# Attention probabilities turned by crossbar DMA as float16 halves, scores and values in float16 halves, two heads side by side in the value products

## The chip, the cores and the metric

The kernel runs on one core of one Trainium2 chip. The metric is the device time of one execution in microseconds (us); lower is better. The core has a matrix engine (PE, with weight loads shown apart as PEld), VectorE (DVE), ScalarE (ACT), GpSimd (POOL) and SyncE (SP), each with its own in-order queue. The kernel issues nearly all of its DMAs from SP.

## What is computed

One layer of a streaming encoder works on 1,024 prompt frames and 32 sample frames of 1,024 channels. The input is normalised, projected by nine weight groups, and goes through two branches: causal attention with 16 heads of 64 channels, and a depthwise convolution of width 31. Both are gated, projected, mixed and projected once more. The part that matters here is the attention of the prompt (the reference, cut):

```python
def fox_attend(q, k, v, cq, ck, qpos, kpos):
    s = jnp.einsum('bqhd,bkhd->bhqk', q.astype(jnp.float32), k.astype(jnp.float32))
    bias = jnp.transpose(cq, (0, 2, 1))[:, :, :, None] - jnp.transpose(ck, (0, 2, 1))[:, :, None, :]
    mask = qpos[:, None] >= kpos[None, :]
    s = jnp.where(mask[None, None], s + bias, jnp.finfo(jnp.float32).min)
    p = jax.nn.softmax(s, axis=-1)
    o = jnp.einsum('bhqk,bkhd->bqhd', p, v.astype(jnp.float32))
    return o.astype(v.dtype)
...
for i in range(T // Q_BLOCK):
    lo, hi = i * Q_BLOCK, (i + 1) * Q_BLOCK
    blocks.append(fox_attend(q[:, lo:hi], k[:, :hi], v[:, :hi], c[:, lo:hi], c[:, :hi],
                             jnp.arange(lo, hi), jnp.arange(hi)))
```

A block of 128 queries `i` of a head looks at the first `128 * (i + 1)` keys, so a head has 36 tiles of 128 queries by 128 keys.

## The kernel before

The program has five stages. First x is normalised and turned. Then come the projections of the convolution input, of v, k, q and of the gate `ga`, with the convolution's taps on DVE (`conv_taps`, L377) between them. Then comes the attention stage, then the output projections "pa" and "pb" (L186, called by `outproj`), then the last product (L1537). A projection multiplies float16 halves: a weight is split into `wh` and `wl`, x into `xh` and `xl`, and each 128x352 output tile collects 8 times 3 matmuls (`mms`, L186).

In the attention stage 22 gate projections (`filler`, `gate_steps`) are woven in as filler: one call of `fill(1)` runs one step of three matmuls (128x352 each), 24 steps make a gate. Each such step is also one beat that paces the taps on DVE and the splitting of the next weights (`wl` on DVE at L144, `wh` on POOL at L139).

The stage goes through a list `seq` of 128 blocks (16 heads of 8 query blocks) and four `Sample` items for the 32 sample frames. For each block:

- `scores` (L1150, L1151): two products into PSUM `psS`, one of 128 rows for the cross terms of the q and k halves (QB, KB) and one of 68 rows for the high halves and the cumulative log gates (QA, KA). The tiles are float32 rounded for the matrix engine. A block of 128 keys is computed 256 wide.
- `top` (L1157, L1159): DVE adds the causal mask to the diagonal tile and takes the row maximum.
- `soft` (L1166): ACT takes the exponential into SBUF tile `P` and sums the rows.
- `norm` (L1171, L1172): DVE takes the reciprocal, POOL scales `P`.
- `turn` (L1186, L1189): PE transposes the 128x128 tiles of `P` in float32 into PSUM; ACT or DVE copies them to the SBUF tiles `pt`.
- `values` (L1205 to L1214): once per head, 20 float32 products 64 channels tall; tile `j` writes the upper or the lower half of the PSUM partitions by whether `j` is even or odd, ACT copies one half and DVE adds the other, and every second head POOL multiplies by the gate `ga`, and the tile goes to DRAM `s_o`.

The order of PE, SP, DVE and ACT in this stage is the order in which the code is written (`manual_schedule`): block `n` is turned while block `n + 3` is scored, with filler after it. q, k and v pass through DRAM in float32 (`s_q`, `s_k`, `s_v`), and `Head.load` brings them back by eight DMAs a head. A DMA on SP uses one of eight semaphores in turn and so waits for the DMA eight places ahead of it.

## Time and profile before

| what | value |
|---|---|
| time, median of 3 runs | 1330.91 us (1329.0, 1330.91, 1336.58) |
| profiled execution, first to last instruction | 1331.8 us |
| granted clock of PE, mean | 0.996 of full |
| busy share PE / DVE / ACT / POOL | 98% / 74% / 52% / 42% |
| attention stage in the trace | 566.5 to 1041.8 us |
| DMA, whole span | 194.96 MB, mean 146 GB/s |

The profiled execution took 1331.8 us from its first to its last instruction; the profile shows nothing around that, and the span lies 0.9 us above the median of the three runs. In the profile a line such as "L186 PE MATMUL pj<-xl,wh" names the line of the kernel, the engine, the operation, and the tile written and the tiles read. Matmuls are pipelined, so the duration of one is longer than the distance to the next; costs on PE are read from the distance between starts.

### The profile page before, as it was taken

To read this page: it belongs to the slowest core of one execution; us is meant where nothing else is said; L and a number is where in the kernel's file an instruction comes from. 1 tells how busy PE (TensorE), PEld (TensorE's weight loads), DVE (VectorE), ACT (ScalarE), POOL (GpSimd) and SP (SyncE) were. 2 spreads that over 40 slices of the span, in tenths; PEclk is the share of its full clock that TensorE was granted. 3 is DMA by queue.
4 is the path that set the end of the run, shared out by engine and by line. 5 is a ranking of instruction groups with operands and counts; after the bars stand their busy time and mean duration, and the time that the engine had idled before them with its cause. 6 is when DMAs were issued, how large, how long until landed. Compare 5 with 4: busy or idle time off the path is not lost.

```text
span 1331.8 us, 24835 instructions
## 1 busy us (share of the span) xinstructions
PE 1311.1 (98%) x9396; PEld 1004.7 (75%) x9396; DVE 986.0 (74%) x1513; ACT 693.1 (52%) x1336; POOL 565.2 (42%) x597
## 2 busy tenths in 40 slices
PE   8999999999999999999899999999999999999999
PEld 5687876666666666677577767767777699999998
DVE  6797879889999998897787875754555388176664
ACT  5644545767686843455545555555555466233320
POOL 4001014637475730245445544342443258255562
PEclk8999999999999999999999999999999999999999
DMA  6243243425252553526545654465561788434461
GB/s 253 99 137 109 86 121 112 146 63 198 86 187 65 186 156 130 164 69 165 147 119 142 181 142 121 114 187 134 150 170 39 247 320 275 157 130 143 126 214 67
DMA packets 113495, 194.96 MB, mean 146 GB/s; under 512 B 34080, under 2 KB 80032, under 8 KB 113376
## 3 DMA queue, kind: packets, MB, share of 16 engines
q1 hardware_dynamic: 113232, 193.31, 46.9%
q8 instruction: 74, 1.21, 0.4%
q14 instruction: 45, 0.37, 0.1%
q10 hardware_dynamic: 144, 0.07, 0.0%
HBM read 127.68 MB, written 65.64 MB: 145 GB/s over the span
## 4 chain that ended last, share of the span: by engine, by line
PE 88%; DVE 7%; ACT 2%; issue 1%; DMA 1%; SPq 1%; POOL 0%; DVEq 0%; ACTq 0%; POOLq 0%
PE pj L186 59%; PE pjv L785 6%; PE pj L1537 6%; PE po L1205 5%; PE ptr L1186 4%; PE psS L1151 2%; PE psS L1150 2%; DVE y L377 2%; DVE wl L144 1%; DVE nm L1159 1%; DMA s_y<-y 1%; PE pst L884 1%; PE pst L885 0%; DMA ga<-s_ga 0%; PE ptx L586 0%
## 5 line engine op out<-in xcount | busy, mean ns | idle before, releaser
L186 PE MATMUL pj<-xl,wh 128*128 128x352 f16 (+2 forms) x1536 | 481.7, 314 | 1.8 <-DVE xl L593 1.6
L186 PE MATMUL pj<-xh,wh 128*128 128x352 f16 (+2 forms) x1536 | 482.2, 314 | 0.8 <-DVE qn L919 0.6
L186 PE MATMUL pj<-xh,wl 128*128 128x352 f16 (+2 forms) x1536 | 481.7, 314 | 0.0
L186 PEld LDWEIGHTS <-wh 128*128 128x128 f16 x3072 | 301.6, 98 | 161.7 <-issue 8.1
L377 DVE SCALAR_TENSOR_TENSOR y<-u,vec_t,y 128x1086 f32<-128x1086 f32 x240 | 348.5, 1453 | 12.1 <-ACT y L374 9.0
L1172 POOL TENSOR_SCALAR P<-P,nm 128x128 f32<-128x128 f32 (+7 forms) x128 | 140.9, 1101 | 203.3 <-DVE nm L1171 181.9
L186 PEld LDWEIGHTS <-wl 128*128 128x128 f16 x1536 | 150.8, 98 | 71.0 <-issue 1.4
L1166 ACT ACTIVATE P<-psS,nm 128x128 f32<-128x128 f32 (+7 forms) x128 | 95.1, 743 | 129.1 <-DVE nm L1171 111.8
L144 DVE SCALAR_TENSOR_TENSOR wl<-raw,sc,wh 128x384 f16<-128x384 f32 x188 | 133.3, 734 | 16.3 <-ACT wh L141 15.8
L1159 DVE TENSOR_REDUCE nm<-psS 128x1 f32<-128x128 f32 (+7 forms) x128 | 97.0, 758 | 10.7 <-POOL P L1172 0.5
L1186 PE MATMUL ptr<-ident,P 128*128 128x128 f32 x576 | 87.2, 274 | 9.8 <-DVE pt L1189 4.7
L1189 ACT COPY pt<-ptr 128x512 f32<-128x512 f32 (+3 forms) x128 | 64.4, 503 | 44.6 <-PE ptr L1186 44.3
L178 POOL TENSOR_TENSOR wl<-raw,wh 128x384 fp32r<-128x384 f32 (+1 forms) x51 | 60.9, 1221 | 61.8 <-ACT wh L175 46.7
L904 POOL TENSOR_TENSOR sql<-sqf,sqh 128x352 fp32r<-128x352 f32 x48 | 57.7, 1203 | 64.9 <-ACT sqh L901 64.9
L1186 PEld LDWEIGHTS ptr<-ident,P 128*128 128x128 f32 x576 | 69.0, 141 | 19.3 <-POOL rstd L357 3.7
L1150 PE MATMUL psS<-KB,QB 128*128 128x256 f32 (+2 forms) x192 | 81.6, 426 | 0.0
L120 POOL CAST topb<-tops 128x2 bf16<-128x2 f32 x35 | 18.6, 532 | 135.9 <-ACT junk L117 86.0
L1205 PE MATMUL po<-pt,V 128*64 128x256 f32 x640 | 72.6, 382 | 2.6 <-ACT pts L1107 2.6
L930 POOL TENSOR_TENSOR ql<-qn,qh 128x352 fp32r<-128x352 f32 (+1 forms) x48 | 67.6, 1424 | 6.1 <-ACT qh L929 6.0
L785 PE MATMUL pjv<-vwh,xh 128*128 128x260 f16 x256 | 70.1, 274 | 0.0
L785 PE MATMUL pjv<-vwl,xh 128*128 128x260 f16 x256 | 70.0, 273 | 0.0
L785 PE MATMUL pjv<-vwh,xl 128*128 128x260 f16 x256 | 69.9, 273 | 0.0
(277 smaller groups left out, 2572.1 us busy)
## 6 DMA issues: line engine op xcount, KB each, us to landing
raw<-wf SPq DMA_DIRECT2D x92, 512.0 KB
QB<-s_q SPq DMA_DIRECT2D x32, 256.0 KB
KB<-s_k SPq DMA_DIRECT2D x32, 256.0 KB
kT<-qn SPq DMA_DIRECT2D x8, 528.0 KB
s_ga<-t SPq DMA_DIRECT2D x24, 176.0 KB
s_gb<-t SPq DMA_DIRECT2D x24, 176.0 KB
s_ma<-t SPq DMA_DIRECT2D x24, 176.0 KB
s_mb<-t SPq DMA_DIRECT2D x24, 176.0 KB
```

The lines of the kernel that those rows point to most:

```text
L144: nc.vector.scalar_tensor_tensor(wl[:, ks, :], raw[:, ks, :], self.s[:, i:i + 1], wh[:, ks, :], op0=ALU.mult, op1=ALU.subtract)
L186: nc.tensor.matmul(ps, a[:, kt, :], b(kt, sl), start=(first and n == 0), stop=(last and n == N - 1))
L377: t = nc.vector.scalar_tensor_tensor(y, u[:, i:i + CW], w, y, op0=ALU.mult, op1=ALU.add)
L785: nc.tensor.matmul(ps[:, :VC], a, b, start=(n == 0), stop=(n == 23))
L930: nc.gpsimd.tensor_sub(ql[:, :n], qn[:, o], f32(qh[:, :n]))
L1150: nc.tensor.matmul(ps[:, b, :wm], QB[:, qsl], KB[:, ksl], start=True, stop=False)
L1159: nc.vector.tensor_reduce(nm[:, 0:1], ps[:, :nb, :w], axis=AX.XY, op=ALU.max, negate=True)
L1166: nc.scalar.activation(P[:, :nk].rearrange("p (b w) -> p b w", b=nb), ps[:, :nb, :w], AF.Exp, bias=nm[:, 0:1], accum_out=nm[:, 1:2])
L1172: nc.gpsimd.tensor_scalar(P[:, :nk], P[:, :nk], nm[:, 2:3], 1.0, op0=ALU.mult, op1=ALU.mult)
L1186: nc.tensor.transpose(pt[:, 128 * j:128 * j + 128], P[:, 128 * (4 * u + j):128 * (4 * u + j) + 128], ident)
L1205: nc.tensor.matmul(po[rows], V[:, j, :], parts[c][:, j, :], start=(c % 2 == 0 and j < 2), stop=(c % 2 == 1 and j >= 2 * c))
L1537: nc.tensor.matmul(pss[c][:, :HC], a[:, k, :], x, start=(not more and kt == 0 and n == 0), stop=(kt == 3 and n == 2), skip_group_check=more)
```

## The change

Everything between q, k, v and the attention output is stored as pairs of float16 halves, high and low. The DRAM copies of q and k become float16. The cumulative log gates become three float16 parts, so that the product of the high halves has 70 rows. A power of two moves between the gains of q and k so that both fit float16 (`gains`, `balance`); k is scaled back for its output (`unscaled`). v is stored as two float16 tensors `vh` and `vl`.

Heads are treated in pairs. A `Unit` is a query block `i` of head `e` of the pair, and 128 units run in the order pair, block, head. `Unit.scores` computes only the keys that exist and adds the causal mask by a matmul with a scaled identity (`identm`, `masks[0]`). After the exponential, `factor` makes the reciprocal times 2^14, `high` (ACT) writes the high half of the scaled probabilities, and `low` writes the low half: by one DVE instruction for the even head, by two POOL instructions for the odd head. `turn` is one DMA per unit that transposes both halves from `PH` to `PT` in the crossbar; there are no transposes on PE and no copies from PSUM. `Pair2.values` makes the products of a pair for 256 queries: three float16 products (high by high, low by high, high by low) for each key tile and each head, with head 0 in PSUM partitions 0 to 63 and head 1 in 64 to 127, one after the other in program order. `gated` scales on ACT and multiplies by the gate on POOL.

The loop issues, for unit `k`: its scores, the factor and high half of unit `k - 1`, half of the filler, its maximum and exponential, the low half of unit `k - 1`, the events of that step (loads, value products, sample work), the other half of the filler, and the transposing DMA of unit `k - 2`. Filler is dealt out in proportion to a unit's width plus 320; 30 of the 528 filler steps are kept for the end. The value products of a pair's block pair `m` stand `LAG` = 5 steps behind its last unit.

The diff, cut to its core (left out are the power of two between q and k, the mask constants, the sample's tile names and the loads of the first heads):

```diff
--- before.py
+++ after.py
...
+PS14 = 2.0 ** 14
+LAG = 5
+WB = 320
...
-    s_q = dram.tile([2, D, T], F32, name="s_q")
-    s_k = dram.tile([2, D, T], F32, name="s_k")
-    s_v = dram.tile([8, 128, D], F32, name="s_v")
+    s_q = dram.tile([2, D, T], F16, name="s_q")
+    s_k = dram.tile([2, D, T], F16, name="s_k")
+    s_v = dram.tile([2, 8, 128, D], F16, name="s_v")
...
-            nc.sync.dma_start(s_v[t, :, 256 * c:256 * c + 256], vf)
+            vh, vl = [vp.tile([128, 256], F16, name=n, tag=n, bufs=3) for n in ("vh", "vl")]
+            vx = vp.tile([128, 256], F32, name="vx", tag="vx", bufs=2)
+            nc.scalar.mul(vh, ps[:, :256], 2.0 ** -15)
+            nc.gpsimd.tensor_scalar(vx, vf, vsc[:, c:c + 1], 1.0, op0=ALU.mult, op1=ALU.mult)
+            nc.gpsimd.tensor_sub(vl, vx, vh)
+            for n, x in enumerate((vh, vl)):
+                nc.sync.dma_start(s_v[n, t, :, 256 * c:256 * c + 256], x)
...
+            (0.5, lambda: V.tensor_scalar(rc, cc, 1.0 / CU, None, op0=ALU.mult)),
+            (0.5, lambda: V.tensor_copy(cp3[:, 0, :], rc)),
+            (0.8, lambda: V.tensor_sub(rc, rc, cp3[:, 0, :])),
+            (0.5, lambda: V.tensor_copy(cp3[:, 1, :], rc)),
+            (0.8, lambda: V.tensor_sub(cp3[:, 2, :], rc, cp3[:, 1, :])),
+            (0.8, lambda: V.tensor_scalar(cn3, cp3, -1.0, None, op0=ALU.mult)),
...
+            ql = tp.tile([128, CH], F16, name="ql", tag="ql")
+            nc.gpsimd.tensor_sub(ql[:, :n], qn[:, o], qh[:, :n])
+            nc.sync.dma_start(dst[0, f * 128:(f + 1) * 128, o], qh[:, :n])
+            nc.sync.dma_start(dst[1, f * 128:(f + 1) * 128, o], ql[:, :n])
+                    kun = tp.tile([128, TT], F32, name="kun", tag="kun", bufs=1)
+                    def unscaled():
+                        nc.scalar.mul(kun, qn, bal[:, 1:2])
+                        nc.sync.dma_start(kT[f], kun)
...
+    class Heads:
...
+                QA, QB, KA, KB = [hp.tile([n, T], F16, name=f"{a}{e}", tag=f"{a}{e}", bufs=2)
+                                  for a, n in (("QA", 70), ("QB", 128), ("KA", 70), ("KB", 128))]
+                for t, src, low, c in ((QB, s_q, 0, s_aq), (KB, s_k, 64, s_ak)):
+                    nc.sync.dma_start(t[low:low + 64], src[1, hs, :])
+                    nc.sync.dma_start(t[64 - low:128 - low], src[0, hs, :])
+                for t, src, c in ((QA, s_q, s_aq), (KA, s_k, s_ak)):
+                    nc.sync.dma_start(t[0:64], src[0, hs, :])
+                    nc.sync.dma_start(t[64:70], c[h])
+                self.q.append((QA, QB, KA, KB))
...
+            self.V = [hp.tile([128, 8, 128], F16, name=n, tag=n, bufs=2) for n in ("Vh", "Vl")]
+            for n, t in enumerate(self.V):
+                nc.sync.dma_start(t, s_v[n, :, :, 128 * self.g:128 * self.g + 128].rearrange("b t d -> t b d"))
...
+    class Unit:
...
-            QA, QB, KA, KB = self.head.q
...
-            ps = psS.tile([128, 2, 512], F32, name="psS", tag="S")
-            nb = 1 if nk <= 512 else 2
-            for b in range(nb):
-                ksl = slice(b * w, b * w + wm)
-                nc.tensor.matmul(ps[:, b, :wm], QB[:, qsl], KB[:, ksl], start=True, stop=False)
-                nc.tensor.matmul(ps[:, b, :wm], QA[:, qsl], KA[:, ksl], start=False, stop=True)
+            self.ps = ps = psS.tile([128, T], F32, name="psS", tag="S")
+            for k0 in range(0, w, 512):
+                ksl = slice(k0, min(k0 + 512, w))
+                last = ksl.stop == w
+                nc.tensor.matmul(ps[:, ksl], QB[:, qsl], KB[:, ksl], start=True, stop=False)
+                nc.tensor.matmul(ps[:, ksl], QA[:, qsl], KA[:, ksl], start=False, stop=not last)
+            nc.tensor.matmul(ps[:, w - 128:w], identm, masks[0], start=False, stop=True)
...
-            diag = ps[:, nb - 1, w - 128:w]
-            nc.vector.tensor_add(diag, diag, cmask)
-            nm = ap.tile([128, 3], F32, name="nm", tag="nm", bufs=6)
-            nc.vector.tensor_reduce(nm[:, 0:1], ps[:, :nb, :w], axis=AX.XY, op=ALU.max, negate=True)
+            self.nm = ap.tile([128, 3], F32, name="nm", tag="nm", bufs=6)
+            nc.vector.tensor_reduce(self.nm[:, 0:1], self.ps[:, :self.w], axis=AX.X, op=ALU.max, negate=True)
...
+        def factor(self):
+            nm = self.nm
             nc.vector.reciprocal(nm[:, 2:3], nm[:, 1:2])
-            nc.gpsimd.tensor_scalar(P[:, :nk], P[:, :nk], nm[:, 2:3], 1.0, op0=ALU.mult, op1=ALU.mult)
+            nc.vector.tensor_scalar(nm[:, 2:3], nm[:, 2:3], PS14, None, op0=ALU.mult)
+
+        def high(self):
+            n = self.i + 1
+            self.H = ap.tile([128, 8, 2, 128], F16, name="PH", tag="PH", bufs=3)
+            self.P3 = self.P[:, :self.w].rearrange("p (j k) -> p j k", j=n)
+            nc.scalar.mul(self.H[:, :n, 0, :], self.P3, self.nm[:, 2:3])
+
+        def low(self):
+            n = self.i + 1
+            f = self.nm[:, 2:3]
+            if self.e:
+                nc.gpsimd.tensor_scalar(self.P3, self.P3, f, 1.0, op0=ALU.mult, op1=ALU.mult)
+                nc.gpsimd.tensor_sub(self.H[:, :n, 1, :], self.P3, self.H[:, :n, 0, :])
+            else:
+                nc.vector.scalar_tensor_tensor(self.H[:, :n, 1, :], self.P3, f, self.H[:, :n, 0, :],
+                                               op0=ALU.mult, op1=ALU.subtract)
 
...
-                pt = psT.tile([128, 512], F32, name="ptr2", tag="T")
-                for j in range(nj):
-                    nc.tensor.transpose(pt[:, 128 * j:128 * j + 128],
-                                        P[:, 128 * (4 * u + j):128 * (4 * u + j) + 128], ident)
...
-                for j in range(2 * c + 2):
-                    rows = slice(64 * (j % 2), 64 * (j % 2) + 64)
-                    nc.tensor.matmul(po[rows], V[:, j, :], parts[c][:, j, :], start=(c % 2 == 0 and j < 2),
-                                     stop=(c % 2 == 1 and j >= 2 * c))
...
+            i, e, m = self.i, self.e, self.i // 2
+            if i % 2 == 0 and e == 0:
+                self.pair.pt[m] = ap.tile([128, 2, 2, 2 * m + 2, 2, 128], F16, name="PT", tag=f"PT{m % 2}", bufs=1)
+            out = self.pair.pt[m][:, i % 2, e, :i + 1, :, :].rearrange("p j n q -> p (j n) q")
+            nc.sync.dma_start_transpose(out, self.H[:, :i + 1, :, :].rearrange("p j n k -> p (j n k)"))
...
+            Vh, Vl = self.hd.V
+            for j in range(2 * m + 2):
+                ii = slice(1 if j == 2 * m + 1 else 0, 2)
+                for n, (v, x) in enumerate(((Vh, 0), (Vl, 0), (Vh, 1))):
+                    for e in range(2):
+                        nc.tensor.matmul(po[64 * e:64 * e + 64, 128 * ii.start:256], v[:, j, 64 * e:64 * e + 64],
+                                         pt[:, ii, e, j, x, :], start=(j == 0 and n == 0),
+                                         stop=(j == 2 * m + 1 and n == 2))
+            self.po = po
...
+    def fill_for(x):
+        share["want"] += x
+        n = int(share["want"]) - share["done"]
+        share["done"] += n
+        fill(n)
+
+    rate = (24 * NFILL - 30) / sum(u.w + WB for u in units)
...
+    for g, p in enumerate(duos):
+        t = 16 * g
+        if g + 1 < len(duos):
+            at(t + 2, duos[g + 1].hd.load)
+            at(t + 5, duos[g + 1].hd.load_v)
+        for m in range(4):
+            k = t + 4 * m + 3 + LAG
+            at(k - 4, lambda p=p, m=m: p.load_gate(m))
+            at(k, lambda p=p, m=m: p.values(m))
...
+    for k in range(len(units) + 2):
+        u = units[k] if k < len(units) else None
+        last = units[k - 1] if 0 < k <= len(units) else None
+        if u:
+            u.scores()
+        if last:
+            last.factor()
+            last.high()
+        fill_for(rate * (u.w + WB) / 2 if u else 2.0)
+        if u:
+            u.top()
+            u.soft()
+        if last:
+            last.low()
+        for fn in events.pop(k, ()):
+            fn()
+        fill_for(rate * (u.w + WB) / 2 if u else 2.0)
+        if k > 1:
+            units[k - 2].turn()
+    for k in sorted(events):
+        fill(5)
+        for fn in events.pop(k):
+            fn()
...
```

PE before, in the attention stage where the scores of a two-tile block stand ahead of the transposes of a seven-tile one (QB, KB, QA, KA are the halves of q and k, P the probabilities, ident the identity, pj the filler's output):

```order
L186 MATMUL pj<-xl,wh 128x352
L1150 MATMUL psS<-KB,QB 128x256
L1151 MATMUL psS<-KA,QA 128x256
L1186 MATMUL ptr_8895<-ident,P 128x128 x4
L1186 MATMUL ptr_8901<-ident,P 128x128 x3
L186 LDWEIGHTS wh
```

PE after, at a unit of two key tiles (`identm` is the scaled identity, `mask` the causal mask):

```order
L190 MATMUL pj<-xl,wh 128x352
L1198 LDWEIGHTS QB_8593
L1198 MATMUL psS<-KB_8595,QB_8593 128x256
L1199 LDWEIGHTS QA_8592
L1199 MATMUL psS<-KA_8594,QA_8592 128x256
L1200 LDWEIGHTS identm
L1200 MATMUL psS<-mask_180,identm 128x128
L190 LDWEIGHTS wh
```

The transposes behind the scores are gone, every score product has a weight load row of its own, and a 128x128 product adds the mask.

SP before, where a head is loaded (raw is a weight tile for the filler, s_ma a gate's output):

```order
L969 DMA s_ma<-t 128x352
L984 DMA QB<-s_q 64x1024
L985 DMA QB<-s_q 64x1024
L986 DMA KB<-s_k 64x1024
L987 DMA KB<-s_k 64x1024
L988 DMA QA<-s_q 64x1024
L989 DMA QA<-s_aq 4x1024
L990 DMA KA<-s_k 64x1024
L991 DMA KA<-s_ak 4x1024
L1194 DMA ga<-s_ga 128x1024
L109 DMA raw<-wf 128x1024
```

SP after, behind the sixteen loads of a pair, of which the last five are shown (PH and PT are the probabilities ahead of and behind the crossbar):

```order
L1038 DMA KB_8595<-s_k 64x1024
L1040 DMA QA_8592<-s_q 64x1024
L1041 DMA QA_8592<-s_aq 6x1024
L1040 DMA KA_8594<-s_k 64x1024
L1041 DMA KA_8594<-s_ak 6x1024
L1238 DMA_TRANSPOSE PT<-PH 128x2x128 x2
L1248 DMA ga<-s_ga 128x256
L1018 DMA s_gb<-t 128x352
L1238 DMA_TRANSPOSE PT<-PH 128x4x128
L1268 DMA s_o<-ot 128x256
L1047 DMA Vh<-s_v 128x8x128
L1047 DMA Vl<-s_v 128x8x128
```

The loads of two heads now stand in one run, and the transposing DMAs of the next units stand behind them in the same queue, between stores and loads.

DVE before, in the later part of the stage (nm holds maximum, sum and reciprocal):

```order
L144 SCALAR_TENSOR_TENSOR wl<-raw,sc,wh 128x384
L1210 TENSOR_TENSOR ot<-ot,po 64x512 x2
L144 SCALAR_TENSOR_TENSOR wl<-raw,sc,wh 128x256
L1157 TENSOR_TENSOR psS<-psS,cmask 128x128
L1159 TENSOR_REDUCE nm<-psS 128x1
L1171 RECIPROCAL nm<-nm 128x1
```

DVE after, at two units (PH is the low half that DVE writes for the even head):

```order
L1214 RECIPROCAL nm<-nm 128x1
L1215 TENSOR_SCALAR nm<-nm 128x1
L1204 TENSOR_REDUCE nm<-psS 128x1
L1230 SCALAR_TENSOR_TENSOR PH<-P,nm,PH 128x6x128
L1214 RECIPROCAL nm<-nm 128x1
```

The mask addition and the copies from PSUM are gone, the reciprocal of unit k - 1, which reads the sum of its exponential, stands ahead of the maximum of unit k, and each second unit has a pass over its probabilities.

257 lines of the change are left out of this document (104 added, 153 removed).

## Prediction

> **What bounds the kernel now.** I read the page's engine totals first, then the busy times by stage, then the issue times of single PE instructions, and last the other engines in the stage that the change touches.
>
> ```profile
> span 1331.8 us, 24835 instructions
> PE 1311.1 (98%) x9396; PEld 1004.7 (75%) x9396; DVE 986.0 (74%) x1513; ACT 693.1 (52%) x1336; POOL 565.2 (42%) x597
> ...
> 46.50:566.50 520.00, 519.45 (x3725) 361.16 (x3724) 458.68 (x526) 303.00 (x558) 193.44 (x192) 1.00 0.41 131
> 566.50:1041.80 475.30, 462.92 (x3458) 336.40 (x3457) 323.47 (x682) 251.19 (x572) 207.68 (x254) 1.00 0.49 134
> 1041.80:1246.70 204.90, 204.90 (x1298) 197.56 (x1299) 116.61 (x134) 89.76 (x119) 103.58 (x79) 1.00 0.60 208
> ```
>
> The columns of the stages are length, busy time of PE, PEld, DVE, ACT and POOL, granted clock, DMA share and GB/s. PE is the bound everywhere. The attention stage is 475.3 us long with 12.4 us in which PE is idle; DVE has 68% of it, ACT 53%, POOL 44%. Work taken off PE there shortens the stage, until DVE or a transfer is in the way. The granted clock is 1.00, so cost is instructions.
>
> Costs on PE come from the distances between starts:
>
> ```profile
> 513.47 21.50 PE pj L186 x144
> 956.57 4.47 PE po L1205 x40
> ...
> 914.46 0.39 PE L1150 MATMUL psS<-KB,QB 128*128 128x512 f32 x1
> 914.69 0.40 PE L1151 MATMUL psS<-KA,QA 68*128 68x512 f32 x1
> 914.93 0.71 PE L1186 MATMUL ptr<-ident,P 128*128 128x128 f32 x5
> 915.48 0.31 PE L186 MATMUL pj<-xh,wh 128*128 128x352 f16 x1
> ...
> L186 PE MATMUL pj<-xh,wh 128*128 128x352 f16 x529 | 166.2, 314 | 0.0
> L1186 PE MATMUL ptr<-ident,P 128*128 128x128 f32 x576 | 87.2, 274 | 9.8 <-DVE pt L1189 4.7 <-ACT pt L1189 2.4 <-DVE os_t L1131 1.5
> L1205 PE MATMUL po<-pt,V 128*64 128x256 f32 x640 | 72.6, 382 | 2.6 <-ACT pts L1107 2.6
> ```
>
> A float16 matmul of 352 columns takes 21.50 / 144 = 0.149 us, 0.424 ns a column. Three times 529 of them in the stage are 237 us of filler, and they stay. A score matmul of 512 columns takes 0.235 us (914.46 to 914.93 for two), 0.459 ns a column. A transpose takes (915.48 - 914.93) / 5 = 0.11 us, so 576 take 63.4 us. A record of the value products takes 4.47 / 40 = 0.112 us, so 640 take 71.5 us.
>
> **The change part by part.** *Transposes.* All 576 leave PE: -63.4 us.
>
> *Scores.* Before, a head has 4,736 columns (blocks below 256 are computed 256 wide) in two products: 9,472 x 0.459 ns = 4.35 us. After, 4,608 columns twice and eight masks of 128 are 10,240 x 0.424 ns = 4.34 us. I count no difference: the narrower blocks pay for the mask.
>
> *Value products.* A pair has 6 x 4,608 = 27,648 float16 columns in 120 matmuls; eight pairs are 221,184 columns. One after the other that is 93.8 us, 22 more than now. Two side by side, in the two halves of the array, it is 46.9. Does the array do that?
>
> ```profile
> 807.23 0.76 PE L1235 MATMUL psn<-mean,ones_f 128*128 128x352 f32 x2
> ...
> 909.23 0.65 PE L1119 MATMUL po<-vc,pts 128*32 128x64 f32 x32
> 909.70 0.29 PE L1119 MATMUL po<-pts 128*32 128x64 f32 x8
> ```
>
> L1235 is float32 at full width: one record lasts 459 ns in its group, so the second starts 0.30 us after the first, 0.85 ns a column. At that rate a 256-column record of L1205 would take 0.218 us; it takes 0.112. The old products, which alternate between the halves too, already run two at a time. I take 46.9: -24.6, with +22 as the other end.
>
> Against this stands the Trainium skill, "TensorE: Matmul & The Clock Gate", section "The mechanism": a weight load overlaps running matmuls only where the row groups differ, and both heads use all rows. By that rule the products would not gain, and the sum would be that of the third rival. The trace doesn't bear it out: L1119 starts 32 products with 32 loads, all on full rows, in 0.47 us, 15 ns each.
>
> PE's work becomes 462.9 - 63.4 - 24.6 = 375 us. With the idle time of now the stage would be 387.
>
> *What is late next: DVE.*
>
> ```profile
> L1159 DVE TENSOR_REDUCE nm<-psS 128x1 f32<-128x128 f32 (+7 forms) x128 | 97.0, 758 | 10.7 <-POOL P L1172 0.5
> L377 DVE SCALAR_TENSOR_TENSOR y<-u,vec_t,y 128x1086 f32<-128x1086 f32 x46 | 67.5, 1466 | 2.3 <-ACT y L374 2.2
> L144 DVE SCALAR_TENSOR_TENSOR wl<-raw,sc,wh 128x384 f16<-128x384 f32 (+1 forms) x66 | 43.9, 683 | 0.4 <-POOL wh L139 0.4
> L1157 DVE TENSOR_TENSOR psS<-psS,cmask 128x128 f32<-128x128 f32 x128 | 37.4, 292 | 28.7 <-PE psS L1151 28.5
> L1189 DVE COPY pt<-ptr 128x128 f32<-128x128 f32 (+1 forms) x64 | 31.2, 488 | 43.9 <-PE ptr L1186 43.7
> L1210 DVE TENSOR_TENSOR ot<-ot,po 64x512 f32<-64x512 f32 x31 | 21.2, 685 | 53.8 <-ACT ot L1209 53.8
> L1171 DVE RECIPROCAL nm<-nm 128x1 f32<-128x1 f32 x128 | 19.7, 154 | 0.1
> ...
> 600.00:700.00 100.00, 93.33 (x705) 66.31 (x702) 77.19 (x141) 50.86 (x115) 48.55 (x54) 0.98 0.55 144
> 700.00:800.00 100.00, 97.95 (x740) 71.52 (x737) 77.89 (x149) 53.61 (x120) 53.49 (x56) 1.00 0.55 153
> ```
>
> DVE loses L1157, L1189 and L1210, 89.8 us. It gains 128 small factors at the 154 ns of L1171, 19.7 us, and 64 low halves of 576 columns on average: 0.78 us each by L377 (1.35 ns a column), 1.03 by L144 (1.78 for 384), so 50 to 66; I take 58. That is 323.5 - 89.8 + 19.7 + 58 = 311 us, 80% of 387. It isn't spread evenly: the 46 taps come at 0.2 a filler step, within 230 of the 528 steps, the first 44%. There DVE has (311 - 67.5) x 0.44 + 67.5 = 175 us against 0.44 x 387 = 170 us of PE. DVE can't be full: the factor of unit k - 1 waits for that unit's exponential on ACT, and the maximum of unit k is queued behind it, as the order shows; ACT's exponential of unit k, and through it the PSUM tile for PE's scores two units on, wait for that. In the first stretch now (600 to 800) DVE is 77 to 78% busy with PE the bound. I take 88%, halfway to 98: 175 / 0.88 = 199 us, 29 more than PE needs. Ends: nothing more than 5 us at 100%, 54 at 78%. So the stage is 387 + 29 = 416, 59 less than before.
>
> *ACT and POOL.*
>
> ```profile
> L1166 ACT ACTIVATE P<-psS,nm 128x128 f32<-128x128 f32 (+7 forms) x128 | 95.1, 743 | 129.1 <-DVE nm L1171 111.8 <-PE ptr L1186 8.8 <-DVE nm L1094 5.2
> L1189 ACT COPY pt<-ptr 128x512 f32<-128x512 f32 (+3 forms) x128 | 64.4, 503 | 44.6 <-PE ptr L1186 44.3
> ...
> L1172 POOL TENSOR_SCALAR P<-P,nm 128x128 f32<-128x128 f32 (+7 forms) x128 | 140.9, 1101 | 203.3 <-DVE nm L1171 181.9 <-DVE sc L160 9.8 <-PE pj L186 7.9
> L1362 POOL TENSOR_TENSOR c_l<-y,c_h 128x1056 fp32r<-128x1056 f32 x8 | 22.9, 2862 | 13.2 <-ACT c_h L1361 13.2
> ```
>
> ACT swaps its copies (64.4) for 128 high halves at the exponential's 743 ns (95), near 282 us. POOL swaps 140.9 for 64 times 1.10 + 1.56 (L1362's 2.71 ns x 576), 170 us. Both stay under 70% of 416 and off the bound: 0.
>
> *The crossbar.* No row shows a transposing DMA. It moves 2 x 36 tiles x 64 KB a pair, 37.7 MB in all.
>
> ```profile
> q1 hardware_dynamic: 113232, 193.31, 46.9%
> ...
> L985 SPq DMA_DIRECT2D QB<-s_q x14: 586/587/1957, 597.1 to 978.3; - x14
> L969 SPq DMA_DIRECT2D s_gb<-t x24: 319/320/735, 571.4 to 739.6; - x24
> ```
>
> The stage's DMA share, 0.49 of 475.3 us at 134 GB/s, is 233 us for 63.7 MB, 273 GB/s while busy. Half-size q and k loads (15 heads x 0.79 MB less) save 43 us and leave 190. Fast end: 37.7 MB at 273 GB/s are 138 us; 328 of 416 then, and nothing waits. Slow end: pieces of 128 float16 elements (256 bytes), 147,456 of them, at the mean packet time of q1, 0.469 x 1331.8 x 16 / 113,232 = 88 ns, are 811 us. I take the fast end, since its rows are of this stage and a mean packet of 1.7 KB is far from a 256-byte one. SP spends 0.32 to 0.59 us on an issue; its 287 other DMAs between the first transpose and the last (counted in the order) are some 126 us at 0.44, and even if it were held for the 138 us it would be busy for 264 of 416. The three steps from turn to product, at 387 / 128 = 3 us each about 9 us, cover landing: 0.
>
> The Trainium skill, "DMA: Bandwidth & Descriptors", section "Latency and other measured facts", gives 261 GB/s for a transposing DMA of scattered pieces. By it the estimate would be 145 us, and the sum the same. No run so far shows it.
>
> *Outside the stage.* The v halves and the rescaled k add passes on ACT and POOL, which have 303 and 193 us of 520 there; PE, the bound, gets nothing. The gains and masks add a dozen small DVE instructions near the start: +2 (0 to 5).
>
> **Sum.** 1331.8 - 59 + 2 = 1275 us, against the profiled execution, which lies 0.9 above the median; the median run doesn't move the number.
>
> **Rivals.**
> - *PE alone stays the bound.* The chain of exponential, factor and maximum hides in the filler, the stage is 387 to 392: 1331.8 - 88 + 2 = 1246 to 1251. For it: ACT and POOL idle half the time. Against: the 175 us of DVE in the first stretch.
> - *DVE becomes the bound throughout.* At the share of now, 68%, 311 us need 457: 1331.8 - 18 + 2 = 1316. For it: each unit's two hops between ACT and DVE. Against: the second half has DVE at 244 - 107 = 136 us of 217.
> - *The value products don't run side by side.* PE 422, with its idle time 434; DVE's excess in the first stretch shrinks to 199 - 191 = 8: 442, so 1300.
> - *The crossbar is the bound: slower.* The DMA engines have 475 - 190 = 285 us for it before the stage is longer than it was, which is 132 GB/s or 31 ns a 256-byte piece. SP's queue is in order, so the weight loads and gate stores behind a held transpose would stop PE as well. At half the mean packet time, 44 ns, it takes 406 us: stage 596, 1331.8 + 121 + 2 = 1455. For it: the smallness of the pieces, and sixteen loads of about 0.5 us ahead of the first transposes of each pair. Against: the pieces go in DMAs of 64 to 512 KB.
> - *It does nothing measurable:* stalls for landings give back all 88 us, over 5 us at each of the 32 value groups: 1331.
>
> **How the numbers follow.** Chances: forecast 0.46 (1255 to 1295), PE alone 0.18, DVE throughout 0.07, products one by one 0.09, no change 0.05, crossbar 0.15. The range from 1244 to 1320 holds the first four, 0.80, and both ends of DVE's cost. About 0.5%, 7 us, is what a measurement here can tell from no change: faster 0.80, same 0.05, slower 0.15.
>
> **What would show it.** The filler's matmuls keep 0.149 us; no PE transposes of P are left; the value records start about 0.05 us apart (0.1 refutes that step); the stage ends near 980 us; in its first 200 us DVE is near 88% busy and PE's idle time is named after the exponential or maximum, and in the second half PE is nearly full. The prediction is wrong if PE waits for PT ahead of the value products, if the DMA share is near 1, or if SP waits behind transposes so that weights come late.

## The result and the profile after

The changed kernel takes 1429.2 us (median of 4 runs, 1425.98 to 1429.69), the kernel before 1332.4 beside it: a ratio of 1.0726 (95% interval 1.0698 to 1.0755). The change makes it 7% slower; 1275 had been predicted, so 154 us were missed. The four runs lie within 3.7 us, and differences between single runs below that size are read as nothing.

Span and engine totals of the changed kernel, then its busy time by stage in the columns of the prediction (length, PE, PEld, DVE, ACT, POOL, granted clock, DMA share, GB/s):

```profile
span 1427.0 us, 24878 instructions
PE 1281.1 (90%) x9270; PEld 944.1 (66%) x9270; DVE 1000.2 (70%) x1494; ACT 733.6 (51%) x1376; POOL 651.4 (46%) x622
...
46.00:566.00 520.00, 519.86 (x3725) 361.25 (x3724) 465.54 (x529) 318.99 (x599) 271.51 (x260) 1.00 0.36 112
566.00:1140.00 574.00, 436.38 (x3353) 278.11 (x3352) 332.41 (x654) 278.59 (x575) 218.90 (x216) 0.89 0.70 160
1140.00:1427.00 287.00, 283.77 (x1952) 277.13 (x1949) 172.47 (x224) 108.35 (x146) 145.02 (x117) 1.00 0.57 184
```

Everything happened in the attention stage: it grew from 475 to 574 us, while the stage ahead is still 520 and what follows 287. No engine is full in it: PE has 76% of the stage, DVE 58%, ACT 49%, POOL 38%, and the DMA engines 0.70. So this is a kernel that waits. Its largest waits in that stage (engine, instruction, what it waited for, us in total, times, longest):

```profile
POOL P L1227 <- ACT PH L1221: 248.2, 56, 18.5
ACT PH L1221 <- DMA PT<-PH: 173.8, 51, 10.2
DVE nm L1214 <- ACT P L1209: 106.0, 51, 10.4
DVE PH L1230 <- ACT PH L1221: 73.5, 43, 8.2
...
PE psS L1198 <- ACT P L1209: 60.4, 38, 6.6
...
PE po L1258 <- DMA PT<-PH: 49.6, 15, 7.5
PEld L1258 <- DMA PT<-PH: 34.5, 9, 7.7
```

The second row is the one to read: it is the largest wait on something other than a compute engine. `high` (L1221) writes `PH`, of which there are three buffers, and unit k's high half needs the buffer that unit k - 3 left. That buffer is free only when the transposing DMA that reads it has landed. ACT runs in order, so behind the blocked high half stand the exponential (DVE's factor waits, third row), and behind that the PSUM tile that PE needs for the next scores (fifth row). The waits of POOL and DVE for L1221 are the same stall seen from there. PE's waits for `PT` at the value products, which the prediction named, are smaller.

Why do the landings come late? SP's queue in the stage shows it (DMA issues and ACT's instructions, start, length):

```profile
713.14 4.12 SPq L1238 DMA_TRANSPOSE PT<-PH  x1
717.36 0.54 SPq L1037 DMA_DIRECT2D QB<-s_q  x1
...
719.50 0.51 ACT L1221 ACTIVATE PH<-P,nm 128x256 f16<-128x256 f32 x1 [8.38 <-DMA PT<-PH]
...
726.15 0.48 SPq L1041 DMA_DIRECT2D KA<-s_ak  x1
726.74 2.49 SPq L1238 DMA_TRANSPOSE PT<-PH  x2
729.19 0.51 ACT L1221 ACTIVATE PH<-P,nm 128x256 f16<-128x256 f32 x1 [8.72 <-DMA PT<-PH]
```

A turn of the longest rows holds SP for 4.12 us, then the sixteen loads of the next pair's q and k hold it from 717.36 to 726.63, and only then the next turns are issued. ACT stands for 8.38 and 8.72 us. Six such bursts stand among the turns, and the ten waits of over 5 us in, right after or right beside one make 84 of the 173.8 us. In the steady part of a pair something else holds SP:

```profile
814.50 1.16 POOL L1228 TENSOR_TENSOR PH<-P,PH 128x512 f16<-128x512 f32 x1
...
816.39 2.78 POOL L143 TENSOR_SCALAR wh<-raw,sc 128x1024 f16<-128x1024 f32 x2
...
819.13 1.75 POOL L1267 TENSOR_TENSOR ot<-ot,ga 128x256 f32<-128x256 f32 x1
...
820.91 0.33 SPq L1268 DMA_DIRECT2D s_o<-ot  x1
821.33 0.38 SPq L1018 DMA_DIRECT2D s_ma<-t  x1
...
821.76 2.73 SPq L1238 DMA_TRANSPOSE PT<-PH  x2
...
825.15 0.94 ACT L1221 ACTIVATE PH<-P,nm 128x768 f16<-128x768 f32 x1 [2.64 <-DMA PT<-PH]
```

The low half is done at 815.66 (spans on POOL are rough). Its turn is issued at 821.76, since SP stands at the output store, that at POOL's gate product, and that behind two weight casts. The turn itself then lands in 3.4 us. SP's own largest waits in the stage are at the two kinds of store, the gates' (L1018) and the output's (L1268):

```profile
SPq L1018 <- ACT t L1017: 93.7, 37, 8.8
SPq L1268 <- POOL ot L1267: 72.7, 31, 6.7
```

The steps that the prediction priced on PE can be read from starts:

```profile
825.22 0.46 PE L1258 MATMUL po<-PT,Vh 128*64 128x256 f16 x4
825.44 0.35 PE L1258 MATMUL po<-PT,Vl 128*64 128x256 f16 x2
...
827.68 0.38 PE L1198 MATMUL psS<-KB,QB 128*128 128x512 f16 x1
827.90 0.38 PE L1199 MATMUL psS<-KA,QA 70*128 70x512 f16 x1
828.12 0.33 PE L1198 MATMUL psS<-KB,QB 128*128 128x384 f16 x1
...
829.10 0.31 PE L190 MATMUL pj<-xh,wl 128*128 128x352 f16 x1
829.25 0.31 PE L190 MATMUL pj<-xl,wh 128*128 128x352 f16 x1
```

Four value records start within 0.22 us, 0.055 each: two at a time. Scores take 0.22 us for 512 columns, the filler 0.15.

### The profile page after: what moved, and what is told of

Read it like the earlier page. It is cut to its first block, busy times and chain, and to the rows that moved or that the text cites. A ratio compares the mean times of both kernels' runs of the same rounds, so it can differ in the third digit from the quotient of the medians.

```text
span 1427.0 us, 24878 instructions
## 1 busy us (share of the span) xinstructions
PE 1281.1 (90%) x9270; PEld 944.1 (66%) x9270; DVE 1000.2 (70%) x1494; ACT 733.6 (51%) x1376; POOL 651.4 (46%) x622
## 5 line engine op out<-in xcount | busy, mean ns | idle before, releaser
L381 DVE SCALAR_TENSOR_TENSOR y<-u,vec_t,y 128x1086 f32<-128x1086 f32 x240 | 353.8, 1475 | 6.2 <-ACT y L378 3.1
L1221 ACT ACTIVATE PH<-P,nm 128x256 f16<-128x256 f32 (+7 forms) x128 | 99.1, 774 | 236.2 <-DMA PT<-PH 173.8
L1227 POOL TENSOR_SCALAR P<-P,nm 128x128 f32<-128x128 f32 (+3 forms) x64 | 54.7, 854 | 251.7 <-ACT PH L1221 248.2
L148 DVE SCALAR_TENSOR_TENSOR wl<-raw,sc,wh 128x384 f16<-128x384 f32 x188 | 142.4, 777 | 25.5 <-ACT wh L145 20.0
L1198 PE MATMUL psS<-KB,QB 128*128 128x512 f16 (+2 forms) x192 | 65.6, 341 | 60.6 <-ACT P L1209 60.4
L1258 PE MATMUL po<-PT,Vh 128*64 128x256 f16 (+1 forms) x640 | 74.6, 312 | 49.7 <-DMA PT<-PH 49.6
L1230 DVE SCALAR_TENSOR_TENSOR PH<-P,nm,PH 128x128 f16<-128x128 f32 (+3 forms) x64 | 64.0, 1001 | 75.8 <-ACT PH L1221 73.5
L1209 ACT ACTIVATE P<-psS,nm 128x256 f32<-128x256 f32 (+7 forms) x128 | 93.4, 730 | 29.3 <-DVE nm L1204 25.4
L1204 DVE TENSOR_REDUCE nm<-psS 128x1 f32<-128x256 f32 (+7 forms) x128 | 95.8, 749 | 10.6 <-PE psS L1200 10.6
L1214 DVE RECIPROCAL nm<-nm 128x1 f32<-128x1 f32 x128 | 20.2, 158 | 106.3 <-ACT P L1209 106.0
L1228 POOL TENSOR_TENSOR PH<-P,PH 128x128 f16<-128x128 f32 (+3 forms) x64 | 86.2, 1347 | 5.2
L1258 PEld LDWEIGHTS <-Vh 128*64 128x64 f16 x640 | 55.7, 132 | 46.1 <-DMA PT<-PH 34.5
```

The costliest lines, as they stand in the source:

```text
L148: nc.vector.scalar_tensor_tensor(wl[:, ks, :], raw[:, ks, :], self.s[:, i:i + 1], wh[:, ks, :], op0=ALU.mult, op1=ALU.subtract)
L381: t = nc.vector.scalar_tensor_tensor(y, u[:, i:i + CW], w, y, op0=ALU.mult, op1=ALU.add)
L1198: nc.tensor.matmul(ps[:, ksl], QB[:, qsl], KB[:, ksl], start=True, stop=False)
L1204: nc.vector.tensor_reduce(self.nm[:, 0:1], self.ps[:, :self.w], axis=AX.X, op=ALU.max, negate=True)
L1209: nc.scalar.activation(self.P[:, :self.w], self.ps[:, :self.w], AF.Exp, bias=self.nm[:, 0:1], accum_out=self.nm[:, 1:2])
L1221: nc.scalar.mul(self.H[:, :n, 0, :], self.P3, self.nm[:, 2:3])
```

## The experiments

Theories: SLOT, ACT waits for one of too few `PH` buffers; QUEUE, the turn is issued late, behind other work of SP; RATE, the crossbar or the DMA engines are too slow for so many small pieces; later CHAIN, exponential, factor, high half and maximum wait for each other whatever the turns do, and HOLD, a turn keeps SP's queue from others or slows the DMA engines for them. Times without an interval are single runs; the kernel before had 1327 to 1332 us beside them.

**e1, the turn earlier in the step.**

```diff
+        if k > 1:
+            units[k - 2].turn()
         if u:
             u.scores()
...
-        if k > 1:
-            units[k - 2].turn()
```

> Only the place of the transposing DMA in SP's queue changes: that of unit k-2 stands at the start of step k instead of its end; all work is kept. Three theories. SLOT: the high half of unit k waits for the landing of the transpose of unit k-3, whose PH buffer it takes (three buffers), and that lands late because it is issued late; a step (about 4 us) of head start then removes most of the 174 us that ACT waits for it, and the time falls to 1370 us or less. RATE: the crossbar cannot turn 37.7 MB faster, wherever the DMA stands; 1415 to 1435. QUEUE: SP is held up by stores that wait for other engines and by the transposes themselves, whatever their order; 1395 to 1425.

Measured: 1394.2, ACT's wait for PH down from 173.8 to 111.7. Nearly a quarter of the loss hangs on where the turn stands. The time is 24 us above SLOT's range and 0.8 below QUEUE's, so none of the three is decided.

**e2, stores off SP's queue.**

```diff
-            nc.sync.dma_start(s_g[g][f, :, sl], t)
+            (nc.scalar if "cast" in sides else nc.sync).dma_start(s_g[g][f, :, sl], t)
...
-            nc.sync.dma_start(s_o[self.hd.g, :, 256 * m:256 * m + 256], ot)
+            nc.gpsimd.dma_start(s_o[self.hd.g, :, 256 * m:256 * m + 256], ot)
```

> In the attention stage the gate stores are issued by ACT, which makes their data, and the stores of the attention output by POOL, which makes theirs, so SP never waits for those two. QUEUE: the transposes and loads behind those stores come earlier, time 1340 to 1385. SLOT: part of it, since the transposes also land earlier, 1385 to 1415. RATE: 1415 to 1435.

Measured: 1385.3, the wait 105.0. On the border of the two ranges. The stores ahead of the turns cost some 44 us. Without them SP stands at the turns themselves: it waits 78 us in the stage for POOL's low half. The median time from a turn's issue to its landing is 4.0 us here.

**e3, about half the tiles turned.**

```diff
-            out = self.pair.pt[m][:, i % 2, e, :i + 1, :, :].rearrange("p j n q -> p (j n) q")
-            nc.sync.dma_start_transpose(out, self.H[:, :i + 1, :, :].rearrange("p j n k -> p (j n k)"))
+            h = i // 2 + 1
+            out = self.pair.pt[m][:, i % 2, e, :h, :, :].rearrange("p j n q -> p (j n) q")
+            nc.sync.dma_start_transpose(out, self.H[:, :h, :, :].rearrange("p j n k -> p (j n k)"))
...
-                                         pt[:, ii, e, j, x, :], start=(j == 0 and n == 0),
+                                         pt[:, ii, e, j % (m + 1), x, :], start=(j == 0 and n == 0),
```

> Each transposing DMA turns only the first i//2+1 of the i+1 key tiles of its unit (20 of 36 tiles of a head); the value products read the turned tiles twice, so PE's work is the same; the output leaves out the other tiles' values. RATE: with 56% of the bytes (-95 us of DMA engine time) the stage is no longer held by the crossbar, 1300 to 1340. SLOT: landings come 1 to 1.5 us sooner for wide units, 1370 to 1400. QUEUE: SP is held 1.2 us instead of 1.56 by a transpose, 1390 to 1415.

**e4, an ordinary copy in place of the transposing DMA.**

```diff
-            nc.sync.dma_start_transpose(out, self.H[:, :i + 1, :, :].rearrange("p j n k -> p (j n k)"))
+            nc.sync.dma_start(out, self.H[:, :i + 1, :, :].rearrange("p j n k -> p (j n) k"))
```

> Each transposing DMA is replaced by a plain SBUF to SBUF copy of the same tile in the same place of the queue, so the probabilities are not turned. RATE: it is the crossbar, and a plain copy of the same bytes brings the forecast of 1275, at most 1310. SLOT and QUEUE: a copy holds SP 0.4 instead of 1.56 us and lands sooner, so part of the wait goes, 1310 to 1380. If it stays above 1400, the transposing itself is not the cost, only a DMA at that place.

Measured: e3 1404.1, e4 1396.8. Turning 20 of 36 tiles gave back 25 us, no transposing at all 32. e3 lies in QUEUE's range; e4 lies 17 us above the range of SLOT and QUEUE and just under the 1400 that was to show that the transposing itself costs nothing. RATE falls as the main cause: 122 of the 154 us stay without the crossbar, and ACT still waits 132.9 us for an ordinary copy, where it waited 173.8 for turns.

```profile
L1238 SPq DMA_DIRECT2D PT<-PH x128: 464/471/1472, 571.6 to 1090.3; - x128
...
  ACT PH L1221: 132.9, 39
  PE po L1258: 45.2, 12
```

These rows of e4 are the issue's length on SP (minimum, median, maximum in ns) and who waited for the landing. A plain issue holds SP for 0.47 us; a transposing one of the changed kernel for more:

```profile
L1238 SPq DMA_TRANSPOSE PT<-PH x128: 1167/1354/4652, 572.2 to 1120.2; - x128
```

**e5, e1 and e2 together.**

> The two edits of e1 (turn of unit k - 2 ahead of step k's scores) and e2 (gate and output stores off SP's queue) together; they saved 35 and 44 us alone. TWO DELAYS (the turn's place in the step and SP's queue are separate, additive delays of the same hand-back of PH): 1340 to 1360, and ACT's wait for PH under 60 us. ONE DELAY (both only shorten the same few waits, or a third wait is behind them): 1370 to 1390, ACT's wait for PH stays near 100 us.

Measured: 1397.5, no better than either; ACT's wait is 93.5. It lies 7 above the range of ONE DELAY, the nearer one. A turn waits on SP for POOL's low half, 64 us in that stage, but in e2 alone that is 78; so why the two savings do not add up stays open.

**e6, a fourth PH buffer.**

```diff
-            self.H = ap.tile([128, 8, 2, 128], F16, name="PH", tag="PH", bufs=3)
+            self.H = ap.tile([128, 8, 2, 128], F16, name="PH", tag="PH", bufs=4)
...
-            self.vc = vc = ap.tile([128, 4, 256], F32, name="vc", tag="vc", bufs=1)
-            nc.sync.dma_start(vc, cv[:, :, 256 * g:256 * g + 256])
...
-            vc, vn, pts = self.vc, self.vn, self.pts
+            pf, vn, pts = self.pf, self.vn, self.pts
...
-                                     vc[:, b, hs] if b < 4 else vn[:, hs], start=(b == 0), stop=(b == 4))
+                                     pf[:, hs] if b < 4 else vn[:, hs], start=(b == 0), stop=(b == 4))
```

> The changed kernel with four PH buffers in place of three, nothing else moved; the room comes from leaving out the load of the cached sample values (the sample rows are multiplied with other data). SLOT (ACT's high half waits for a buffer that comes back one step too late): a step is about 4.4 us and the mean of the 51 waits is 174 / 51 = 3.4 us, so most of them go: 1300 to 1345, ACT's wait for PH under 50 us. QUEUE (the turn itself comes late, behind SP's other waits, and lateness adds up): the buffer only puts the same wait off to the value products: 1385 to 1425, PE's wait for PT grows.

Measured: 1389.4, ACT's wait 87.7, PE's for PT 53.8 (49.6 with three). QUEUE's range; a buffer more halves ACT's waits and doesn't end them.

**e7 and e8, turning on PE in float32, split on the way out of PSUM,** for the odd heads (e7) and for all (e8).

```diff
+            if e:
+                for u in range(0, i + 1, 4):
+                    n = min(4, i + 1 - u)
+                    pt = psT.tile([128, 512], F32, name="ptr2", tag="T")
+                    for j in range(n):
+                        nc.tensor.transpose(pt[:, 128 * j:128 * j + 128], self.P3[:, u + j, :], ident)
+                    p3 = pt[:, :128 * n].rearrange("p (j q) -> p j q", j=n)
+                    h, l = [self.pair.pt[m][:, i % 2, e, u:u + n, x, :] for x in range(2)]
+                    nc.scalar.copy(h, p3)
+                    nc.vector.tensor_sub(l, p3, h)
+                return
```

`high` then has nothing to do for these heads, and `low` only scales `P` on POOL, as before the change.

> The odd head of each pair is turned on PE in float32 as before the change and split into halves as it is copied out of PSUM; the even head keeps the crossbar. PE gets back half of the transposes, about 32 us, so PE's own floor is 1331.8 - 88 + 32 = 1276. SLOT (three PH buffers now last for six units): no wait of ACT for PH is left, 1285 to 1320. If what costs time is the landing itself (SP's order, or each transfer's own time before the value products): PE still waits for PT, 1350 to 1400.

> All probabilities are turned on PE in float32 and split into float16 halves as they are copied out of PSUM; scores and value products stay as changed. PE's floor is 1331.8 - 25 = 1307 (only the value products' gain is left). CROSSBAR PATH (the whole loss is the crossbar's path: buffers, order, landing): 1295 to 1325, just faster than before. HALVES (ACT's and DVE's work on the halves carries part of the loss; DVE has 128 low halves out of PSUM now): 1340 to 1400, with PE waiting for PT from DVE.

Measured: e7 1366.6, e8 1448.9. In e7 ACT waits for landings for only 15 us in all, as SLOT said, but the time is 47 us above SLOT's range and in the other one, 1350 to 1400. The reason given for that range fits only in part: PE waits for PT for 27 us, but for DVE's copies, and 9 for landings. In e8 there is no crossbar, and it is slower than the changed kernel and above both of its ranges. Waits of e8 between 560 and 1140 us:

```profile
DVE PT L1247 <- ACT PT L1246: 201.3, 132, 4.4
ACT P L1209 <- DVE nm L1204: 192.7, 103, 10.8
```

DVE's low half waits for ACT's high half of the same tile, and ACT's exponential for the maximum that stands behind it on DVE. So a chain between ACT and DVE may cost as much as the crossbar did. That made CHAIN a theory of its own.

**e9, no turns in seven of eight pairs; e10, the same in another order.** e9's edit in `turn` (the first pair keeps its tiles in `kept`), then e10's in the loop over steps:

```diff
+            if self.pair is not duos[0]:
+                self.pair.pt[m] = duos[0].kept[2 + m % 2]
+                return
```

```diff
-        if last:
-            last.factor()
-            last.high()
         fill_for(rate * (u.w + WB) / 2 if u else 2.0)
         if u:
             u.top()
             u.soft()
         if last:
+            last.factor()
+            last.high()
+        if last and last.e:
             last.low()
+        if k > 1 and not units[k - 2].e:
+            units[k - 2].low()
```

> The changed kernel with the turns left out in seven of the eight pairs; their value products read the tiles that the first pair turned, so the other heads' outputs are those of the first pair's probabilities. Everything else, halves and scores too, is as changed. CROSSBAR (the whole loss hangs on the turns: buffers of PH, SP's order, landing): 1275 plus the first pair's eighth of the 150 us missed, 1285 to 1310. CHAIN (the exponential, the factor, the high half and the maximum wait for each other in the order in which ACT and DVE run them; e7, with little waiting for landings, was 1366, of which 32 are PE's transposes): 1325 to 1355, with ACT waiting for DVE's maximum and DVE for ACT's exponential.

> e9 with the steps in another order: in step k the maximum and the exponential of unit k come first, then factor and high half of unit k - 1, whose exponential is long done, and the low half of the even head one step later. CHAIN: the waits between ACT and DVE go, 1275 to 1310, 20 or more below e9. CROSSBAR: the order matters nothing without the turns, within 8 us of e9.

Measured: e9 1318.3, e10 1304.5. **This is the run that divides the loss.** Without the turns of seven pairs 111 of the 154 us are gone, so most of it hangs on the crossbar's path; the first pair's turns are still in e9, at 111 / 7 = 16 us by the same rate. The other 27 stay without turns. e9 lies between the two ranges, and e10's order gives 14 us, less than CHAIN wanted and more than CROSSBAR allowed; these 14 are what is shown of CHAIN. A part of the stage in e9, the whole stage, and PE's largest wait in it:

```profile
700.00:800.00 100.00, 86.35 (x731) 55.72 (x730) 86.15 (x150) 58.11 (x120) 50.85 (x46) 0.97 0.42 122
...
566.00:1029.50 463.50, 400.83 (x3356) 260.20 (x3354) 338.81 (x657) 280.63 (x576) 222.69 (x217) 0.96 0.45 127
...
PE psS L1198 <- ACT P L1209: 48.9, 33, 4.3
```

Without turns PE and DVE are both 86% busy between 700 and 800. PE has 63 us of idling left in the stage, most of it for the PSUM tile that the exponential holds. One link of that chain, in the changed kernel:

```profile
830.50 1.85 DVE L381 SCALAR_TENSOR_TENSOR y<-u,vec_t,y 128x1086 f32<-128x1086 f32 x1
830.67 1.01 ACT L1209 ACTIVATE P<-psS,nm 128x896 f32<-128x896 f32 x1 [0.47 <-DVE nm L1204]
...
832.27 2.00 DVE L148 SCALAR_TENSOR_TENSOR wl<-raw,sc,wh 128x384 f16<-128x384 f32 x1
...
834.18 0.15 DVE L1214 RECIPROCAL nm<-nm 128x1 f32<-128x1 f32 x1
834.37 0.15 DVE L1215 TENSOR_SCALAR nm<-nm 128x1 f32<-128x1 f32 x1
...
834.61 1.04 ACT L1221 ACTIVATE PH<-P,nm 128x896 f16<-128x896 f32 x1 [2.39 <-issue]
```

The exponential ends at 831.7, but its factor stands behind a tap (L381) and a weight half (L148) until 834.18; ACT's next high half is 2.39 us late.

**e11, e10's order in the changed kernel,** turns and all.

> The changed kernel, turns and all, with e10's order of the steps. CHAIN and CROSSBAR in series (each holds the steps apart): 1380 to 1405, ACT's wait for PH stays above 100 us. CHAIN as the first cause (late halves make late turns): 1320 to 1365, ACT's wait for PH under 60 us. CROSSBAR alone: 1415 to 1440.

Measured: 1404.5, ACT's wait 128.1. As both in series would have it, at the upper edge.

**e12, e7 with e10's order and e2's stores.**

> e7 (odd heads turned on PE in float32 and split on the way out of PSUM, even heads by crossbar) with e10's order, the gate stores issued from ACT's queue and the output stores from POOL's. CHAIN: e7's 139 us of ACT behind the maximum go to a large part: 1310 to 1340. If the bound is DVE's own work (1017 us of the span in e7): 1350 to 1370.

Measured: 1394.6, outside both ranges and slower than e7. DVE waits 134 us for ACT's copies out of PSUM here (48 in e7). e12 changes the order and the stores together; e19 below, 17 us slower than e18, shows for the order alone that what helps one way of turning can hurt the other.

**e13 and e14, turns that nobody waits for.** In pairs 1 to 7 the value products read the first pair's tiles as in e9, and a DMA of the same size goes from `xh` to spare room; e14 makes it an ordinary copy.

```diff
+            if self.pair is not duos[0]:
+                self.pair.pt[m] = duos[0].kept[3]
+                spare = duos[0].kept[2].rearrange("p a e j n q -> p (a e j n) q")
+                o = 16 * ((2 * i + e) % 3)
+                src = xh.rearrange("p t n -> p (t n)")[:, :2 * self.w]
+                nc.sync.dma_start_transpose(spare[:, o:o + 2 * i + 2, :], src)
+                return
```

> e9 (value products of pairs 1 to 7 read the first pair's turned tiles), but the 112 turns are issued all the same, in their places on SP and in their sizes: they read the split input x, which nobody rewrites, and write spare tiles that nobody reads. So SP is held and the DMA engines carry the pieces, while no engine waits for a landing and no PH buffer depends on one. WAITS (the loss is ACT's wait for PH and PE's for PT): 1318 to 1335. HOLD (the loss is SP, held by each turn, so that weights, gates and stores behind it come late, or DMA engines that are slower for everybody): 1390 to 1430. Between 1350 and 1375 each has half.

> e13 with ordinary copies of the same bytes in place of the 112 transposing DMAs: the same traffic, issued without transposing. HOLD: 40 or more below e13, near 1325. WAITS: within 10 of e13, both at 1318 to 1335.

Measured: e13 1349.6, e14 1322.4. e13 lies between its two ranges, and the 27 us between the two runs lie between WAITS' 10 and HOLD's 40. With the others they make a ladder:

| step | from, to | us |
|---|---|---|
| waits for landings | changed 1429.2, e13 1349.6 | 80 |
| HOLD: a turn in place of a copy | e13 1349.6, e14 1322.4 | 27 |
| the traffic | e14 1322.4, e9 1318.3 | 4 |

The ordinary copies give the same two terms along the other side: 1396.8 - 1322.4 = 74 for the waits (e4, e14), 1429.2 - 1396.8 = 32 for HOLD. The 80 include what SP waits for the halves themselves, since `xh` is there from the start. The 4 are no more than single runs differ by. The 27 and the 32 are near each other, but they fall on different waits. In e13 PE stands at the sample's values for a load that SP issued late:

```profile
PE po L1169 <- DMA pts<-s_vs: 21.8, 3, 11.4
```

That wait is 3.3 us in e14 and absent in the changed kernel; from the changed kernel to e4 it is ACT's wait for `PH` that falls, by 41 us. The stretch from 800 to 900 us in e13, then in e14:

```profile
800.00:900.00 100.00, 79.70 (x643) 51.00 (x642) 64.57 (x140) 56.06 (x122) 39.85 (x43) 0.90 0.88 199
...
800.00:900.00 100.00, 87.50 (x735) 56.34 (x732) 72.91 (x166) 66.21 (x145) 45.27 (x49) 0.97 0.68 212
```

Transposing costs the DMA engines 0.88 of the time where copies at a higher rate take 0.68. That is slow, but not full. So HOLD is two things here, SP held longer and busier DMA engines, and these runs don't separate them.

**e15, all that gives a landing slack:** e10's order, e2's stores, e6's fourth buffer, and the value products a step later (`LAG = 6`).

> The changed kernel, all probabilities turned by crossbar, with all that gives slack to a landing: e10's order of the steps, gate and output stores off SP's queue, a fourth PH buffer (the cached sample values are left out for its room, as in e6), and the value products one step later. WAITS: each of these gives a step or takes a delay away, ACT's wait for PH under 30 us and PE's for PT under 30: 1310 to 1345. HOLD: SP is still held, 1370 to 1400.

Measured: 1374.6, within HOLD's range; by the ladder, 1349.6 with HOLD, the order's 14 off, some 39 us of waits are left, as an estimate. They are these (ACT in e15):

```profile
717.05 0.61 ACT L1219 ACTIVATE PH<-P,nm 128x384 f16<-128x384 f32 x1 [8.05 <-DMA PT<-PH]
...
845.83 0.61 ACT L1219 ACTIVATE PH<-P,nm 128x384 f16<-128x384 f32 x1 [11.77 <-DMA PT<-PH]
```

Seven such waits, in or right after one of the six bursts of sixteen loads on SP (704.89 to 714.5 ahead of the first row), make 57 of its 80.5 us. One buffer and one step don't cover a queue that is closed for 9.6 us. Taking those loads off SP was not tried.

**e17, e18, e19, the float16 halves turned on PE.** e18 undoes the crossbar alone, e19 adds e10's order, e17 has the even heads by crossbar and e10's order.

```diff
+            if e:
+                for u in range(0, i + 1, 4):
+                    n = min(4, i + 1 - u)
+                    pt = psT.tile([128, 8, 128], F16, name="ptr3", tag="T")
+                    for j in range(2 * n):
+                        nc.tensor.transpose(pt[:, j, :], self.H[:, u + j // 2, j % 2, :], ident16)
+                    (nc.vector.tensor_copy if u else nc.scalar.copy)(out[:, 2 * u:2 * u + 2 * n, :], pt[:, :2 * n, :])
+                return
```

> The even head of each pair by crossbar; the odd head's two float16 halves are transposed on PE and copied out of PSUM, the first four key tiles by ACT, the others by DVE; steps in e10's order. Three PH buffers last for six units, and no copy waits for another, as e7's low halves did. e10 without turns was 1304; 32 us of transposes on PE and a quarter of the crossbar's 111 us are to be added, less what hides. WAITS: 1315 to 1340. If copies in ACT's and DVE's queues lengthen the step as in e7: 1350 to 1375.

> The crossbar undone and nothing else: the float16 halves of all heads are transposed on PE (1,152 transposes of 128 columns, about 63 us) and copied out of PSUM by ACT and DVE. Scores, halves, value products and the order of the steps are as changed. If PE's transposes fill time in which PE now waits: 1318 - 16 + 63 - 40 = 1325, from 1310 to 1340. If they come on top of the waits between ACT and DVE: 1360 to 1385.

> e18 with e10's order of the steps. CHAIN: 10 to 30 below e18, so 1300 to 1330 or 1340 to 1370 by e18's two cases; if DVE's and ACT's copies bind instead, within 8 of e18.

Measured: e17 1389.4 (ratio to before 1.0436, 1.0366 to 1.0506), e18 1388.7 (1.0431, 1.0349 to 1.0512), e19 1406.0 (1.056, 1.0478 to 1.0643). All are above their ranges. Waits in e18's stage:

```profile
DVE PT L1244 <- PE ptr L1243: 90.2, 46, 6.0
...
ACT PH L1221 <- DVE nm L1215: 60.1, 58, 3.1
...
ACT P L1209 <- DVE nm L1204: 36.8, 38, 8.8
```

Turning on PE instead adds copies in the queues of ACT and DVE, and they wait for PE and for each other, as these rows show. So in no version that turns its probabilities, with the crossbar or without, do the halves pay: none beats the kernel before. Only e9, e10 and e14, which leave the turning out, are below it, by 8 to 23 us in single runs.

## Why the prediction was wrong

*The crossbar, costed at nothing, is the step that failed.* The prediction put it so: "328 of 416 then, and nothing waits", and "the three steps from turn to product [...] cover landing: 0". It counted the time from the turn to the value products, and that read is indeed the smaller wait. It did not count the other one that waits for the landing, the high half three units later that writes the same `PH` buffer, though the count of three is in the code; and it took SP's load as a sum (264 of 416) where SP is a queue whose order decides. The runs put 111 us there: about 80 are waits for landings, and 27 to 32 come of turns in place of copies, on SP and the DMA engines together. Each of the two delays was in reach: the sixteen loads ahead of the first turns of a pair stand in the prediction, as a point for a rival.

*Value products and scores: right.* 0.055 us between value records where 0.05 was forecast and 0.1 would have refuted it; scores and filler as priced. No transposes of P are left on PE. The rule of the Trainium skill, "TensorE: Matmul & The Clock Gate", section "The mechanism", by which loads on the same row groups would not overlap, was set aside on the trace; the changed kernel's 0.055, two records in the time of one, bears that out.

*PE's work: too low.* PE is busy for 436 us in the stage, not 375, and for 401 in e9, where it waits less. Part of that is the granted clock, 0.89 and 0.96 there (last section), which the forecast took as 1.00.

*DVE as the next late engine: the mechanism is seen, the size stays open.* 29 us were put on it, from 5 to 54. With turns out of the way, DVE's 86% between 700 and 800 is close to the 88 forecast, and PE's largest wait is for the exponential, as forecast. But the stage of e9, 463.5 us where 416 were forecast, has 26 us more of PE's busy time (401, not 375) and 22 more of idling (63, not 41), with some 16 of all that from the first pair's turns, by the rate above. What of the rest is DVE's can't be told; e10's order gives 14 back. DVE itself is busy for 332 us in the changed kernel's stage, 311 forecast.

*ACT, POOL, outside: right.* ACT has 278.6 us in the stage (282 forecast), and the stages ahead of it and behind moved by under 4 us. POOL's two instructions of the odd head are 55 + 86 = 141 us where 170 were forecast. What POOL costs would lie not in its load but in its order, as in the rows with the gate product behind the casts.

*The rival "crossbar bound" had the right side, 1455, and half the mechanism.* It needed 31 ns a piece; the stage's DMA share, 0.70 of 574 us less the 190 us of other traffic that the prediction worked out, leaves 212 us where the forecast took 138, 23 ns a piece, as an estimate. The rate is not the bound, as e3 and e4 show. Its other sentence, that SP's queue is in order, was the truth in it; what it saw stuck behind the turns was weights and gates, and in the changed kernel it was the turns that stood behind the rest. The Trainium skill, "DMA: Bandwidth & Descriptors", section "Latency and other measured facts", gives 261 GB/s for transposing with a non-contiguous middle dimension; 37.7 MB in those 212 us are 178 GB/s, as an estimate and with other traffic beside it.

*The rival of no change* has a slip in its working: 88 us over 32 value groups are 2.75 each, not over 5. Nothing else hangs on it.

*Left open:* whether loads off SP's queue would bring the crossbar version under the kernel before (even e10, with nearly no turns, is only 23 us under the 1327.5 beside it); how HOLD divides between SP and the DMA engines; and how e18's loss divides between the added copies and PE's added work.

## What to carry to other kernels

When work moves from an engine to a DMA, ask who waits for the buffer that the DMA reads, not only for the one it writes: count its buffers against the longest time for which the issuing queue can be closed, here 9.6 us of loads against steps of 4.5. A queue's load says little; list what stands ahead of the critical issue in order, and who has to finish before each. And split a loss by experiments that keep one property of a transfer each (turn or copy, traffic, dependence), since removing delays one at a time (e1, e2, e5) does not add up.
